# Float32r warm-up products, and a list scheduler's prices set to measured ones, in a one-core decoder layer

## The chip, the cores and the metric

The kernel runs on one core of a Trainium2 chip. The metric is the device time of one execution in microseconds (us), lower is better; a comparison goes by the median of several executions. TensorE (PE) multiplies matrices into PSUM, VectorE (DVE), ScalarE (ACT) and GpSimd (POOL) do elementwise work, and SyncE (SP) issues most of the DMA transfers.

## The reference

One decoder layer over 256 positions of width 1024, all in float32: four groups of attention heads in parallel, cross attention into 256 memory tokens, a squared-ReLU MLP, and a last norm.

```python
def hybrid_mixer(h, w_in, g_group, sinks, w_out, rel_table):
    proj = (h @ w_in).astype(jnp.float32)
    ...
    ya = dilated_attention(heads(aq), heads(ak), heads(av), rel_table)
    yb = stick_breaking_attention(heads(bq), heads(bk), heads(bv))
    yc = sliding_window_sink_attention(heads(cq), heads(ck), heads(cv), sinks, rel_table)
    yd = moba_attention(heads(dq), heads(dk), heads(dv), rel_table)
    groups = []
    for y in (ya, yb, yc, yd):
        y = y.transpose(0, 2, 1, 3).reshape(B, S, -1)
        groups.append(y * lax.rsqrt(jnp.mean(y * y, axis=-1, keepdims=True) + NORM_EPS))
    y = jnp.concatenate(groups, axis=-1) * g_group.astype(jnp.float32)
    return y.astype(h.dtype) @ w_out

def reference(x, mem, rel_table, g_mix, w_in, g_group, sinks, w_out, g_cross, g_mem,
              w_xq, w_xkv, w_xo, g_mlp, w_up, w_down, g_final):
    for l in range(DEPTH):
        x = x + hybrid_mixer(rmsnorm(x, g_mix[l]), w_in[l], g_group[l], sinks[l], w_out[l], rel_table)
        x = x + memory_cross_attention(rmsnorm(x, g_cross[l]), rmsnorm(mem, g_mem[l]),
                                       w_xq[l], w_xkv[l], w_xo[l])
        x = x + squared_relu_mlp(rmsnorm(x, g_mlp[l]), w_up[l], w_down[l])
    return rmsnorm(x, g_final)
```

## The kernel before

All weights stream from HBM once, in units of 256 columns or rows, each in two transfers of 512 KB into one of four `raw` tiles (line 299, issued by SyncE). ScalarE copies a raw tile to float32r (`hi`, line 313), VectorE subtracts that from the raw one (`lo`, line 314), and each product is made of three float32r products, hi·hi, hi·lo and lo·hi (`mm3`, lines 420 to 422). The raw tile is free again when both have read it, and only then can SyncE load the next weight into it.

The order of work on every engine comes from a planner written in Python (`Plan`). Each call of `pe`, `act`, `dve`, `pool` or `dma` adds an operation with an engine, a price in us, what it reads and what it writes. `arrange` simulates the engines: in each step it looks for each engine at the operations whose inputs are there, takes those that could start within a small slack of the earliest, and among them the one of highest rank. The rank is the length of the chain that hangs on it (level plus boost), or a fixed number. The result is one static order for each engine. `FIRST` holds the plan time at which each engine can begin. Two tags, `raw` and `w`, are handed out strictly in the order in which their tiles were made (`FIFO`). At run time each engine works through its own order and waits by semaphores, so a price that is wrong moves the order, and not the work.

At the start, x arrives in two halves of 128 rows (`load_x`). TensorE transposes each half (line 403), VectorE multiplies by the gain (line 413), and ScalarE and VectorE split the result (lines 396, 397). Until x is there, TensorE runs `WARM` products on a zeroed tile (`warm_up`, line 365), whose rank is -1, so that they only fill holes; nothing reads them. They are there for TensorE's clock. The norm's factor is made in parallel: a sum of squares on ScalarE (line 388), a small operation on VectorE (line 382), and a power of -0.5 on GpSimd (line 383, in `rstd_of`). For the two halves of x the factors are spread over all partitions by two transposes (line 455), and ScalarE makes `rk` and `rq` of them (lines 458, 459), with which q and k of every head group are scaled (line 506).

The first head group's values go by line 491, one product at a time, so that each half of x and each half of the weight can be used as it comes. Its q and k (units aq, ak) and all other projections go by `proj_T` and `proj`. The next head group's q (unit bq) follows. Scores are line 633 for the first 128 queries and lines 600 and 601 for the others, the probabilities are transposed by line 535 and multiplied with the values by line 553. GpSimd writes the biases' strip to DRAM (line 469) and reads it back skewed (`toeplitz`, line 713). From about 160 us on the MLP runs alone.

Of the kernel before, what the change touches and what calls it, by code (L numbers as in the profile page):

```python
# [11 lines left out]
F32 = mybir.dt.float32  # L12
F32R = mybir.dt.float32r
# [14 lines left out]
MLP_RANK = 20.0  # L28
LEAD = 0.6
NPRE = 1  # L30
WARM = 30
FRONT = 20.0
EARLY = 1.0
NUDGE = 0.5
# [51 lines left out]
class Plan:  # L86
# [3 lines left out]
    CROSS = 0.2  # L90
    FIFO = ("raw", "w")
    DMA = 0.95
    FIRST = {"DMA": 1.7, "PE": 1.1, "ACT": 0.6, "DVE": 0.6, "POOL": 0.6}
    REFILL = 1.1
    SLACK = {"DVE": 0.3, "ACT": 0.4, "PE": 0.15}
    IDLE = 50.0
# [118 lines left out]
def trunk(ctx: ExitStack, tc: tile.TileContext, a: dict, out: bass.AP):  # L215
# [124 lines left out]
    load("av", 0)  # L340
    load_x(1)
    load("av", 1)
    ident, mhalf, warm = buf("ident", [P, P]), buf("mhalf", [P, 1]), buf("warm", [P, 512], BF16)
    pool(0.5, lambda: make_identity(nc, ident.t), [], [ident])
    pool(0.05, lambda: nc.gpsimd.memset(mhalf.t, -0.5), [], [mhalf])
    dve(512, lambda: nc.vector.memset(warm.t, 0.0), [], [warm])
    onehot, rel, smask = buf("q", [32, STRIP], F32, 2), buf("rel", [32, NROW]), buf("k", [NROW, STRIP], F32, 2)
    sink, nsink = buf("sink", [P, 4]), buf("nsink", [P, 4])
    pool(0.05, lambda: nc.gpsimd.memset(rel.t, 0.0), [], [rel])
# [10 lines left out]
    def warm_up(n):  # L360

        wps = acct()
        plan.fixed = -1.0
        for _ in range(n):
            pe(0.11, lambda: nc.tensor.matmul(wps[:, 0:P], warm[:, 0:P], warm[:, 0:P], start=True, stop=True), [warm], [wps])
        plan.fixed = None

    warm_up(WARM)
# [8 lines left out]
    gains_T(0)  # L377


    def rstd_of(ssq, n):  # L380
        v, r = buf("var", [P, 1], F32, 4), buf("rstd", [P, 1], F32, 16)
        dve(1, lambda: nc.vector.tensor_scalar(v.t, ssq.t, 1.0 / n, EPS, op0=ALU.mult, op1=ALU.add), [ssq], [v])  # L382
        pool(0.5, lambda: nc.gpsimd.tensor_tensor(r.t, v.t, mhalf.t, op=ALU.pow), [v, mhalf], [r])  # L383
        return r

    def rstd_row(src, view, n):
        sq, ssq = buf("sq", [P, D], BF16, 1), buf("ssq", [P, 1], F32, 4)
        act(n, lambda: nc.scalar.activation(sq[:, 0:n], view(), AF.Square, accum_out=ssq.t), [src], [sq, ssq], 1)
        return rstd_of(ssq, n)

    def pair(tag, n, bufs):
        return tuple(buf(tag + x, [P, n, S], F32R, bufs) for x in ("hi", "lo"))
# [36 lines left out]
    def proj_T(dst, view, u, i, hT):  # L429

        for k in range(KB):
            w, j = wt(u, k)
            pe(0.327, lambda w=w, j=j, k=k: mm3(view(), both(w, ALL, j, tsl(i)), both(hT, ALL, k, ALL), k == 0, k == KB - 1),
               [*w] + [(z, (t, k // 4)) for z in hT for t in range(2)], [dst])

    def proj(dst, view, u, hT, t):

        for k in range(KB):
            w, j = wt(u, k)
            pe(0.327, lambda w=w, j=j, k=k: mm3(view(), both(hT, ALL, k, tsl(t)), both(w, ALL, j), k == 0, k == KB - 1),  # L440
               [*w] + [(z, (t, k // 4)) for z in hT], [dst])


# [1 line left out]
    r1 = []  # L445
    for t in range(2):
        gained_T(xt[t], 0, h1, t)
        r1.append(rstd_row(xt[t], lambda t=t: xt[t].t, D))

    rq, rk = buf("rq", [P, S]), buf("rk", [P, S])  # L450
    pr = pst()
# [20 lines left out]
    def project(gi):  # L472
        n = "abcd"[gi]
        q, k = buf("q", [P, 2, S], F32, 2), buf("k", [P, 2, S], F32, 2)
        names = (n + "q", n + "k" if gi != 2 else "ckv")
        v = buf("v4", [P, 2, 4, E + 1], F32, 2) if gi != 2 else buf("v2", [P, 2, 2, E + 1])
        pool(0.1, lambda: nc.gpsimd.memset(v[:, :, :, E:E + 1], 1.0), [], [(v, 0), (v, 1)])

        def values():
            if gi:  # L480
                load(n + "v")
            for t in range(2):
                pv = acct()
                if gi:
                    proj(pv, lambda pv=pv: pv[:, 0:256], n + "v", h1, t)
                else:
                    for half in range(2):
                        for p in ((0, 0), (1, 0), (0, 1)):
                            for kk in range(4 * half, 4 * half + 4):
                                w, j = wt("av", kk)  # L490
                                pe(0.109, lambda p=p, kk=kk, w=w, j=j, t=t, pv=pv: nc.tensor.matmul(
                                    pv[:, 0:256], h1[p[0]][:, kk, tsl(t)], w[p[1]][:, j], start=kk == 0 and p == (0, 0),
                                    stop=kk == KB - 1 and p == (0, 1)), [w[p[1]], (h1[p[0]], (t, half))], [pv])
                act(256, lambda t=t, pv=pv: nc.scalar.activation(
                    v[:, t, :, 0:E], pv[:, 0:256].rearrange("p (h e) -> p h e", h=4), AF.Copy, scale=r1[t].t),
                    [pv, r1[t]], [(v, t)], 1)

        if gi == 0:
            values()
        for u, z, r in zip(names, (q, k), (rq, rk)):  # L500
            if u != "aq":
                load(u)
            acc = acct()
            for i in range(2):
                proj_T(acc, lambda acc=acc, i=i: acc[:, i * S:(i + 1) * S], u, i, h1)
            dve(512, lambda z=z, r=r, acc=acc: nc.vector.tensor_tensor(
                z.t, acc.t.rearrange("p (i t) -> p i t", i=2), r[:, None, :].to_broadcast([P, 2, S]), op=ALU.mult),
                [acc, r], [z])
        if gi == 2:
            pt = pst()  # L510
            transpose(pt, k, lambda: k[:, 1, :], 2, [k])
            for t in range(2):
                act(128, lambda t=t: nc.scalar.activation(
                    v[:, t, :, 0:E], pt[:, tsl(t)].rearrange("p (g e) -> p g e", g=2), AF.Copy), [pt], [(v, t)])
        elif gi:
            values()
        return q, k, v
# [25 lines left out]
    def weigh(pT, v, kv, vkeys):  # L543

        py = pst()

        def view():
            return py[:, 0:4 * (E + 1)].rearrange("p (h e) -> p h e", h=4)

        for h in range(4):  # L550
            def go(h=h):
                for j, (z, i) in enumerate(pT[h]):
                    nc.tensor.matmul(view()[:, h, :], z[:, i, :], v[:, j, kv(h), :], start=j == 0, stop=j == len(pT[h]) - 1)  # L553
            pe(0.205 * len(pT[h]), go, [z for z, _ in pT[h]] + vkeys, [py])
        return py, view

    def divided(py, view, extra=None):
# [51 lines left out]
    def attend(gi, t, q, k, v, yT):  # L609
# [7 lines left out]
        if t:  # L617
            ks, qs = stack_k(k, lambda: k.t, 1 if gi == 2 else 2), stack_q(q, lambda: q[:, :, tsl(1)])
            for half in range(2):
                def go(half=half):  # L620
                    for h in range(4):
                        qi, ki, hf = place(h)
                        if hf == half:
                            stacked(zv(half, qi), qs, 2 * qi + half, ks, 2 * ki + half)
                pe(0.436, go, [*qs, ks], [pz[half]])
        else:
            def go():
                for i in range(2):
# [70 lines left out]
    def rows_mm(acc, hl, u, t, c0, c1, first, last):  # L699

        for j in range(2):
            w, k = wt(u, j)
            pe(0.65 * (c1 - c0) / 512, lambda w=w, k=k, j=j: mm3(
                acc[:, 0:c1 - c0], both(hl, ALL, j, tsl(t)), both(w, ALL, k, slice(c0, c1)), first and j == 0, last and j == 1),
               [*w] + [(z, t) for z in hl], [acc])

# [63 lines left out]
    for t in range(2):  # L770
# [15 lines left out]
        for half in range(2):  # L786
            def go(half=half, pzs=pzs, qs=qs):
                for g in range(2):
                    stacked(pzs[half][:, g * S:(g + 1) * S], qs, 2 * g + half, kx, 2 * g + half)
            pe(0.436, go, [*qs, kx], [pzs[half]])  # L790
        for half, pz in enumerate(pzs):
            dve(512, lambda half=half, pz=pz, nm=nm: nc.vector.tensor_reduce(
                nm[:, half::2], pz.t.rearrange("p (g s) -> p g s", g=2), axis=mybir.AxisListType.X, op=ALU.min),
# [136 lines left out]
```

## Time and profile before

| | us |
|---|---|
| median of 3 runs | 351.68 |
| lowest, highest | 351.62, 352.77 |
| the profiled execution | 352.86 |
| its span, first to last instruction | 350.9 |

The profiled execution is one of its own, 1.2 us above the median; 1.96 us of it lie around the span. PE is busy for 339.3 us, the loads of its stationary operand (PEld) for 313.8 us, DVE for 230.2 us, ACT for 193.8 us and POOL for 25.8 us. A row of the timeline gives the start in us, the duration in us of all instructions that were merged into it, the engine, line, operation, output and inputs, and the count; brackets behind it hold the idle time of the engine just before, and what ended it. Matmuls overlap in the array, so the time from one to the next is the duration of a row less the length of one, divided by the count less one.

### The profile page before, as it was taken

Reading aid. Unit: us, or ns where it says so; the run is one execution under the profiler, and the core shown is the slowest. Engines: PE = TensorE matmul, PEld = TensorE weight load, DVE = VectorE, ACT = ScalarE, POOL = GpSimd, SP = SyncE. Lnnn points to the kernel's source line nnn. Section 1 sums busy time; section 2 is a strip of 40 time slices with the busy share of each in tenths; the row PEclk is TensorE's granted clock in tenths of the full one; section 3 lists DMA queues with packets and bytes.
Section 4 is the critical chain, followed back from the end, with each engine's and each line's share of the span. In section 5 each row is a group of like instructions: output and inputs, shape, how many; then the busy total and the mean of one; then the engine's idle time right before and its main releaser. Section 6 shows DMA issues by size and latency. Waiting matters only on the chain.

```text
span 350.9 us, 6140 instructions
## 1 busy us (share of the span) xinstructions
PE 339.3 (97%) x2442; PEld 313.8 (89%) x2442; DVE 230.2 (66%) x370; ACT 193.8 (55%) x313; POOL 25.8 (7%) x46
## 2 busy tenths in 40 slices
PE   7898999999999999999999999999999999999992
PEld 6798999999898889988999999999999999999982
DVE  3855879589996699788764645555464644555254
ACT  6576857378893467866644443535344443535132
POOL 6440000000201005000100000000000000000000
PEclk9999999999999999999999999999999999999998
DMA  8998574730156435832647554655647555562003
GB/s 269 335 333 248 163 217 143 241 121 0 63 177 183 122 119 180 269 122 91 223 140 238 179 183 145 216 191 181 196 157 235 182 179 155 205 224 78 2 0 120
DMA packets 39900, 59.88 MB, mean 171 GB/s; under 512 B 2006, under 2 KB 33040, under 8 KB 39872
## 3 DMA queue, kind: packets, MB, share of 16 engines
q1 hardware_dynamic: 39216, 57.69, 51.3%
q0 software_dynamic: 640, 1.80, 1.6%
q8 instruction: 19, 0.31, 0.4%
q14 instruction: 9, 0.07, 0.1%
q10 hardware_dynamic: 16, 0.00, 0.0%
HBM read 58.42 MB, written 1.07 MB: 170 GB/s over the span
## 4 chain that ended last, share of the span: by engine, by line
PE 79%; DVE 6%; DMA 6%; ACT 4%; issue 2%; SPq 0%; POOLq 0%; POOL 0%; DVEq 0%; ACTq 0%
PE acc L420 13%; PE acc L421 13%; PE acc L422 13%; PE ps L421 11%; PE ps L422 11%; PE ps L420 11%; DMA raw<-in_w_in_dram 4%; PE ps L553 3%; PE ps L403 3%; DMA x<-in_x_dram 2%; DVE w L314 2%; ACT ks L581 1%; PE ps L535 1%; ACT w L673 1%; ACT qs L593 1%
## 5 line engine op out<-in xcount | busy, mean ns | idle before, releaser
L314 DVE TENSOR_TENSOR w<-raw,w 128x1024 fp32r<-128x1024 f32 x100 | 120.5, 1222 | 85.0 <-ACT w L313 81.6
L313 ACT ACTIVATE w<-raw 128x1024 fp32r<-128x1024 f32 x100 | 103.5, 1057 | 94.2 <-PE ps L421 43.1
L421 PE MATMUL ps<-hTlo,w 128*128 128x256 f32 x256 | 72.0, 281 | 0.0
L420 PE MATMUL ps<-hThi,w 128*128 128x256 f32 x256 | 71.9, 281 | 0.0
L422 PE MATMUL ps<-hThi,w 128*128 128x256 f32 x256 | 71.9, 281 | 0.0
L420 PE MATMUL acc<-w,yThi 128*128 128x512 f32 (+1 forms) x168 | 64.1, 381 | 0.0
L422 PE MATMUL acc<-w,yTlo 128*128 128x512 f32 (+1 forms) x168 | 62.7, 373 | 0.0
L421 PE MATMUL acc<-w,yThi 128*128 128x512 f32 (+1 forms) x168 | 62.6, 373 | 0.0
L420 PEld LDWEIGHTS ps<-hThi,w 128*128 128x128 f32 x256 | 48.2, 188 | 0.1
L422 PEld LDWEIGHTS ps<-hThi,w 128*128 128x128 f32 x256 | 48.3, 189 | 0.0
L421 PEld LDWEIGHTS ps<-hTlo,w 128*128 128x128 f32 x256 | 48.1, 188 | 0.1
L422 PEld LDWEIGHTS acc<-w,yTlo 128*128 128x128 f32 x168 | 31.5, 188 | 6.2
L422 PE MATMUL acc<-hThi,w 128*128 128x256 f32 x128 | 36.0, 281 | 1.0 <-DVE w L314 1.0
L420 PE MATMUL acc<-hThi,w 128*128 128x256 f32 x128 | 36.6, 286 | 0.0
L421 PEld LDWEIGHTS acc<-w,yThi 128*128 128x128 f32 x168 | 31.6, 188 | 5.4
L420 PEld LDWEIGHTS acc<-w,yThi 128*128 128x128 f32 x168 | 31.6, 188 | 5.3
L421 PE MATMUL acc<-hTlo,w 128*128 128x256 f32 x128 | 36.1, 282 | 0.0
L422 PEld LDWEIGHTS acc<-hThi,w 128*128 128x128 f32 x128 | 24.2, 189 | 1.4 <-DVE w L314 1.4
L383 POOL TENSOR_TENSOR rstd<-var,mhalf 128x1 f32<-128x1 f32 x16 | 14.9, 932 | 143.2 <-DVE var L382 99.2
L420 PEld LDWEIGHTS acc<-hThi,w 128*128 128x128 f32 x128 | 24.1, 188 | 0.4
L421 PEld LDWEIGHTS acc<-hTlo,w 128*128 128x128 f32 x128 | 24.1, 188 | 0.0
L834 ACT ACTIVATE q<-ps 128x512 f32<-128x512 f32 x15 | 9.0, 600 | 11.8 <-PE ps L422 11.8
(152 smaller groups left out, 519.0 us busy)
## 6 DMA issues: line engine op xcount, KB each, us to landing
raw<-in_w_up_dram SPq DMA_DIRECT2D x32, 512.0 KB, 3.9
raw<-in_w_down_dram SPq DMA_DIRECT2D x32, 512.0 KB, 3.9
raw<-in_w_in_dram SPq DMA_DIRECT2D x22, 512.0 KB, 5.0
raw<-in_w_out_dram SPq DMA_DIRECT2D x8, 512.0 KB, 3.4
raw<-in_w_xkv_dram SPq DMA_DIRECT2D x4, 512.0 KB, 3.6
w<-dstrip POOLq DMA_DIRECT2D x3, 512.0 KB, 9.2
x<-in_x_dram SPq DMA_DIRECT2D x2, 512.0 KB, 5.9
tmp<-in_mem_dram SPq DMA_DIRECT2D x2, 512.0 KB, 5.5
```

The costliest lines, as they stand in the source:

```text
L313: act(1024, lambda raw=raw, hi=hi: nc.scalar.activation(hi.t, raw.t, AF.Copy), [raw], [hi])
L314: dve(1024, lambda raw=raw, hi=hi, lo=lo: nc.vector.tensor_sub(lo.t, raw.t, hi.t.bitcast(F32)), [raw, hi], [lo])
L383: pool(0.5, lambda: nc.gpsimd.tensor_tensor(r.t, v.t, mhalf.t, op=ALU.pow), [v, mhalf], [r])
L403: nc.tensor.transpose(dst[:, tsl(k)], view()[:, tsl(k)], ident.t)
L420: nc.tensor.matmul(dst, lh, rh, start=start, stop=False)
L421: nc.tensor.matmul(dst, lh, rl, start=False, stop=False)
L422: nc.tensor.matmul(dst, ll, rh, start=False, stop=stop)
L535: nc.tensor.transpose(pt[:, tsl(i)], w[:, h, tsl(j)], ident.t)
L553: nc.tensor.matmul(view()[:, h, :], z[:, i, :], v[:, j, kv(h), :], start=j == 0, stop=j == len(pT[h]) - 1)
L581: act(n * S, lambda own=own, at=at: nc.scalar.activation(ks[own, at, :], view()[own, 0:n, :], AF.Copy), [k], [(ks, half)])
L593: act(256, lambda r=r, own=own, at=at: nc.scalar.activation(qs[r, at, :], view()[own], AF.Copy), [q], [(qs, half)])
L834: act(512, lambda: nc.scalar.activation(r.t, pu.t.rearrange("p (i t) -> p i t", i=2), AF.Relu), [pu], [r])
```

## The change

The warm-up products are of float32r, 128 columns, and there are 15 of them, not 30. The tile that they read is 128 x 128 of float32r and not 128 x 512 of bf16, and its memset is priced accordingly. In the planner's table, a warm-up product is priced at 0.213 for 0.11; three products of 256 columns at 0.355 for 0.327, of 512 columns at 0.70 for 0.65; a single one at 0.1185 for 0.109; scores at 0.48 for 0.436; a product with the values at 0.224 for 0.205. The first transfer can begin at 2.0 for 1.7. The power on GpSimd is priced at 1.0 for 0.5, and for the two halves of x at 1.5 and 3.0. The last norm's power (line 889) stays at 0.5. The prices of ScalarE and VectorE stay.

```diff
-WARM = 30
+WARM = 15
...
-    FIRST = {"DMA": 1.7, "PE": 1.1, "ACT": 0.6, "DVE": 0.6, "POOL": 0.6}
+    FIRST = {"DMA": 2.0, "PE": 1.1, "ACT": 0.6, "DVE": 0.6, "POOL": 0.6}
...
-    ident, mhalf, warm = buf("ident", [P, P]), buf("mhalf", [P, 1]), buf("warm", [P, 512], BF16)
+    ident, mhalf, warm = buf("ident", [P, P]), buf("mhalf", [P, 1]), buf("warm", [P, P], F32R)
...
-    dve(512, lambda: nc.vector.memset(warm.t, 0.0), [], [warm])
+    dve(128, lambda: nc.vector.memset(warm.t.bitcast(F32), 0.0), [], [warm])
...
-            pe(0.11, lambda: nc.tensor.matmul(wps[:, 0:P], warm[:, 0:P], warm[:, 0:P], start=True, stop=True), [warm], [wps])
+            pe(0.213, lambda: nc.tensor.matmul(wps[:, 0:P], warm.t, warm.t, start=True, stop=True), [warm], [wps])
...
-    def rstd_of(ssq, n):
+    def rstd_of(ssq, n, cost=1.0):
...
-        pool(0.5, lambda: nc.gpsimd.tensor_tensor(r.t, v.t, mhalf.t, op=ALU.pow), [v, mhalf], [r])
+        pool(cost, lambda: nc.gpsimd.tensor_tensor(r.t, v.t, mhalf.t, op=ALU.pow), [v, mhalf], [r])
...
-            pe(0.327, lambda w=w, j=j, k=k: mm3(view(), both(w, ALL, j, tsl(i)), both(hT, ALL, k, ALL), k == 0, k == KB - 1),
+            pe(0.355, lambda w=w, j=j, k=k: mm3(view(), both(w, ALL, j, tsl(i)), both(hT, ALL, k, ALL), k == 0, k == KB - 1),
...
-        r1.append(rstd_row(xt[t], lambda t=t: xt[t].t, D))
+        r1.append(rstd_row(xt[t], lambda t=t: xt[t].t, D, 1.5 * t + 1.5))
...
-                                pe(0.109, lambda p=p, kk=kk, w=w, j=j, t=t, pv=pv: nc.tensor.matmul(
+                                pe(0.1185, lambda p=p, kk=kk, w=w, j=j, t=t, pv=pv: nc.tensor.matmul(
...
-            pe(0.205 * len(pT[h]), go, [z for z, _ in pT[h]] + vkeys, [py])
+            pe(0.224 * len(pT[h]), go, [z for z, _ in pT[h]] + vkeys, [py])
...
-                pe(0.436, go, [*qs, ks], [pz[half]])
+                pe(0.48, go, [*qs, ks], [pz[half]])
...
-            pe(0.65 * (c1 - c0) / 512, lambda w=w, k=k, j=j: mm3(
+            pe(0.70 * (c1 - c0) / 512, lambda w=w, k=k, j=j: mm3(
```

The same two new prices stand in `proj` (0.355) and in the scores of the cross attention (0.48).

## Rows read from the trace of the kernel before

**Rows 1.** Busy time by stage; the first row names the columns.
```profile
core 0: us, PE busy (x) PEld busy (x) DVE busy (x) ACT busy (x) POOL busy (x), PEclk, DMA share, GB/s
0.00:29.00 29.00, 26.03 (x195) 24.11 (x196) 16.29 (x27) 17.82 (x28) 13.32 (x27) 1.00 0.96 315
35.00:160.00 125.00, 123.81 (x937) 114.91 (x936) 104.51 (x208) 85.50 (x167) 9.88 (x13) 1.00 0.50 153
160.00:338.00 178.00, 178.00 (x1238) 164.93 (x1237) 97.02 (x106) 82.32 (x101) 1.42 (x4) 1.00 0.51 165
```

**Rows 2.** Timeline of TensorE, start to 11 us.
```profile
1.18 2.74 PE L365 MATMUL acc<-warm 128*128 128x128 bf16 x24 [1.18 <-DVE warm L346]
4.39 1.09 PE L403 MATMUL ps<-ident,x 128*128 128x128 f32 x4 [0.47 <-DMA x<-in_x_dram]
...
6.52 0.85 PE L365 MATMUL acc<-warm 128*128 128x128 bf16 x6
7.63 1.97 PE L403 MATMUL ps<-ident,x 128*128 128x128 f32 x8 [0.26 <-DMA x<-in_x_dram]
9.25 1.07 PE L491 MATMUL acc<-w,hThi 128*128 128x256 f32 x4
10.25 0.81 PE L467 MATMUL ps<-q,rel 32*13 32x384 f32 x2
```

**Rows 3.** Lengths of single products in ns (min/median/max; mean), and later transposes.
```profile
L403 PE MATMUL ps<-ident,x x48: 270/273/477, 4.4 to 164.4; 128*128 128x128 f32 x48
...
L467 PE MATMUL ps<-q,rel 32*13 32x384 f32 x2 | 0.8, 485 | 0.0
...
114.68 1.03 PE L403 MATMUL ps<-ident,tmp 128*128 128x128 f32 x8
```

**Rows 4.** Where TensorE waits in the front, by the timeline.
```profile
17.15 0.32 PE L455 MATMUL ps<-ident,rstd 128*128 128x128 f32 x1 [1.06 <-POOL rstd L383]
...
29.96 0.38 PE L422 MATMUL acc<-hThi,w 128*128 128x256 f32 x1 [0.47 <-DVE w L314]
...
33.02 0.39 PE L422 MATMUL acc<-hThi,w 128*128 128x256 f32 x1 [0.54 <-DVE w L314]
```

**Rows 5.** Timeline of GpSimd, its first two powers.
```profile
7.67 1.41 POOL L383 TENSOR_TENSOR rstd<-var,mhalf 128x1 f32<-128x1 f32 x1 [2.22 <-DVE var L382]
...
14.06 3.04 POOL L383 TENSOR_TENSOR rstd<-var,mhalf 128x1 f32<-128x1 f32 x1
```

**Rows 6.** Timeline of ScalarE, 27 us to 36 us.
```profile
27.59 1.06 ACT L313 ACTIVATE w<-raw 128x1024 fp32r<-128x1024 f32 x1 [1.48 <-DMA raw<-in_w_in_dram]
30.64 1.06 ACT L313 ACTIVATE w<-raw 128x1024 fp32r<-128x1024 f32 x1 [2.00 <-DMA raw<-in_w_in_dram]
...
34.23 1.26 ACT L673 ACTIVATE w<-w,nm 128x128 f32<-128x128 f32 x4
```

**Rows 7.** The chain that ended last, from 16 us: start us, us, what.
```profile
16.68 13.88 DMA raw<-in_w_in_dram
```

**Rows 8.** Timeline of VectorE, start to 30 us.
```profile
0.85 0.27 DVE L346 MEMSET warm<- 128x256 uint32 x1 [0.85 <-PEq L918]
5.92 1.53 DVE L413 TENSOR_TENSOR tmp<-ps,gT 128x512 f32<-128x512 f32 x2 [4.80 <-ACT gT L375]
...
7.43 1.22 DVE L314 TENSOR_TENSOR w<-raw,w 128x1024 fp32r<-128x1024 f32 x1
...
13.18 3.47 DVE L314 TENSOR_TENSOR w<-raw,w 128x1024 fp32r<-128x1024 f32 x3
...
29.82 0.69 DVE L506 TENSOR_TENSOR k<-acc,rk 128x512 f32<-128x512 f32 x1
```

**Rows 9.** Timeline of TensorE: products of 256 columns, and the first scores.
```profile
17.68 0.28 PE L420 MATMUL acc<-hThi,w 128*128 128x256 f32 x1
...
18.03 0.28 PE L420 MATMUL acc<-hThi,w 128*128 128x256 f32 x1
...
30.98 0.72 PE L633 MATMUL ps<-k,q 64*128 64x128 f32 x8
```

More of the change, by code (lines that the diff above doesn't have):

```diff
@@ L377, in trunk, with rstd_row @@
     gains_T(0)
-    def rstd_of(ssq, n):
+    def rstd_of(ssq, n, cost=1.0):
         v, r = buf("var", [P, 1], F32, 4), buf("rstd", [P, 1], F32, 16)
         dve(1, lambda: nc.vector.tensor_scalar(v.t, ssq.t, 1.0 / n, EPS, op0=ALU.mult, op1=ALU.add), [ssq], [v])
-        pool(0.5, lambda: nc.gpsimd.tensor_tensor(r.t, v.t, mhalf.t, op=ALU.pow), [v, mhalf], [r])
+        pool(cost, lambda: nc.gpsimd.tensor_tensor(r.t, v.t, mhalf.t, op=ALU.pow), [v, mhalf], [r])
         return r
-    def rstd_row(src, view, n):
+    def rstd_row(src, view, n, cost=1.0):
         sq, ssq = buf("sq", [P, D], BF16, 1), buf("ssq", [P, 1], F32, 4)
         act(n, lambda: nc.scalar.activation(sq[:, 0:n], view(), AF.Square, accum_out=ssq.t), [src], [sq, ssq], 1)
-        return rstd_of(ssq, n)
+        return rstd_of(ssq, n, cost)
     def pair(tag, n, bufs):
@@ L439, in proj @@
             w, j = wt(u, k)
-            pe(0.327, lambda w=w, j=j, k=k: mm3(view(), both(hT, ALL, k, tsl(t)), both(w, ALL, j), k == 0, k == KB - 1),
+            pe(0.355, lambda w=w, j=j, k=k: mm3(view(), both(hT, ALL, k, tsl(t)), both(w, ALL, j), k == 0, k == KB - 1),
                [*w] + [(z, (t, k // 4)) for z in hT], [dst])
@@ L789, in go @@
                     stacked(pzs[half][:, g * S:(g + 1) * S], qs, 2 * g + half, kx, 2 * g + half)
-            pe(0.436, go, [*qs, kx], [pzs[half]])
+            pe(0.48, go, [*qs, kx], [pzs[half]])
         for half, pz in enumerate(pzs):
```

## The prediction

> **What bounds the kernel now.** I read the table of stages first [rows 1]: from 160 us to 338 us TensorE is busy without a gap, and from 35 us to 160 us it lacks 1.2 us. Busy time is modelled, but no order of work can gain much there. What is left lies in the first 35 us, in the gaps of the attention stages, and in the last 13 us, which hold the output's scaling and store and are not touched.
>
> In the front, three things are to be seen. First, TensorE runs at half pace until about 10 us, though the granted clock of that stretch is given as 1.00 [rows 1]. Four transposes of x take 1.09 us there [rows 2]; eight take 1.03 us at 114.7 us. [...] Second, TensorE stands still for 1.1 us before line 455, waiting for the rstd of the second half of x from GpSimd [rows 4, 5]. Third, it waits at 29.96 us and 33.02 us for a split weight tile, 0.5 us each [rows 4], which comes late because ScalarE had to wait for the transfer (1.48 us and 2.00 us) [rows 6]. The chain of waits says the same: one transfer from 16.68 us to its landing 13.88 us later [rows 7]. It is slow because the DMA engines are full, with a share of 0.96 over the first 29 us [rows 1].
>
> **The change, part by part. Warm-up.** Thirty bf16 products go, fifteen of float32r come. The old ones: 24 in 2.74 us, 0.11 us each [rows 2]. No row shows a float32r product of 128 columns. The low end is the bf16 one, 0.11 us. The high end is that it costs as a plain f32 product: line 467 makes one of 384 columns in two instructions of 0.485 us, both in 0.81 us, so 0.325 us apart and 0.65 us a product, just after the pace had doubled [rows 2, 3]; a third of it is 0.22 us, at half pace 0.43 us. The value I take is 0.213 us: four f32 transposes, of the same shape and word, go at that pace in the same stretch. Fifteen are then 3.2 us. The memset before them writes 128 words a row, not 256 (0.27 us now [rows 8]), so they start about 0.1 us sooner, at 1.1 us, and end at 4.3 us. x lands at about that time (its transposes start at 4.39 us) [rows 2]. So the fifteen fit into the hole, and the path gets 0. At 0.11 us they leave a hole of 1.6 us, also 0. At 0.43 us they last until 7.5 us, and that is a rival below.
>
> The six products at 6.52 us have no successor, since all fifteen are used up. TensorE is idle there until the second half of x lands at 7.6 us [rows 2]: 0 on the path.
>
> **Clock.** In the kernel before, the pace doubled between 9.3 and 10.3 us, with the first real products of line 491: four of 256 columns in 1.07 us, over 0.2 us each [rows 2], and later such a product takes 0.118 us [rows 9]. With denser warm-up it may come sooner: then the eight transposes at 7.63 us take 1.03 us and not 1.97 us [rows 2, 3], 0.9 us less. It may come later: each product of line 491 costs 0.1 us more while it lasts. I take 0; the ends are -0.9 us and +2.8 us (28 products), both ahead of holes of 1.3 us and 1.5 us that swallow most of it.
> [...]
>
> **Prices of GpSimd.** The planner took 0.5 us for a pow. The rows say 1.41 us and 3.04 us for the two halves of x [rows 5]. Both lie under VectorE's line 314: three of them from 13.18 us to 16.65 us, and the pow, issued at 14.06 us, ends at 17.10 us, 0.45 us behind them; the first one ends 0.43 us behind the line 314 that runs to 8.65 us [rows 5, 8]. So the new 1.5 and 3.0 are mostly the neighbour's length, and hold as long as VectorE's order there stays.
>
> With 3.0 the planner knows that line 455 can't run at 16 us. Its TensorE list has the rest of line 491 and 48 products of aq to put ahead (the first is issued at 17.68 us [rows 9]), so the stall goes: 1.06 us idle [rows 4] and the restart of the pipe, 0.27 us [rows 3], 1.3 us. The waits behind it, rk and rq on ScalarE, are not needed until aq is done, 48 x 0.118 = 5.7 us on.
>
> **What is late next.** After aq and ak (96 products at 0.118 us [rows 9], 11.3 us) TensorE needs bq, whose halves reach ScalarE at 27.59 us and 30.64 us [rows 6]. No byte of that is cheaper now, and the DMA engines are full. The 1.3 us therefore go into a longer wait for bq, but for what else can run in it: the scores of line 633 (eight instructions in 0.72 us, now at 30.98 us [rows 9]; 0.6 us of it on TensorE's path). Their k was copied behind line 314 of bq, at 29.82 us [rows 8]; with ak done 1.3 us earlier it is copied ahead of it. The rest of that head group needs ScalarE, which sits in order behind bq's second half until 31.7 us [rows 6]. So I count -0.6 us, with ends 0 and -1.3 us.
>
> **Prices of TensorE.** Three products of 256 columns cost 0.35 us (17.68 us to 18.03 us) [rows 9], and the table now says 0.355 for 0.327; so the filler that the planner puts ahead of a dependent product is true to length, 8% shorter in count. ScalarE and VectorE stay cheap: four of line 673 take 1.26 us, 0.31 us each [rows 6], where the table has 0.24; a line 314 in a run of three takes 1.16 us [rows 8] for 1.14. For the two attention stages, 35 us to 160 us, the table of stages leaves 1.2 us of TensorE idle [rows 1]. A truer TensorE can remove some, a shorter cover can add some: I take 0, with ends -1.2 us and +3 us (the working is with the rival). The rest (later pows at 1.0, DMA first at 2.0 for 1.7) moves plan times by a few tenths; the first x does land as the 2.0 has it: 2.0 + 1.46 + 0.95 = 4.4 us beside 4.39 us [rows 2].
>
> **Sum.** The profiled execution has a span of 350.9 us in 352.86 us; the median is 351.68 us. 350.9 - 0.6 = 350.3 us of span, 352.3 us for such an execution, and 351.1 us at the median.
>
> **Rivals.** (a) *The front moves as a whole.* If the new order also frees the raw tiles sooner, or puts bq's transfer ahead of those of mem or bias, the 1.3 us stay, the two holes of 0.5 us and their restarts (0.27 us of pipe each, so 1.5 us) [rows 3, 4] shrink, and half of the 1.2 us in attention goes: -1.3 - 1.0 - 0.6 = -2.9 us, 348.8 us. For it: the table now carries the length of the stall at line 455. Against it: the full DMA engines.
> (b) *Shorter cover.* From the scores at 30.98 us to the end of the four exponentials at 35.5 us [rows 6, 9] a head group's chain through VectorE and ScalarE takes 4.5 us; with the transposes, values and norm behind it I estimate 9 us. Its filler loses 8%, 0.7 us. Eight such chains of the four groups and two of the cross attention stand between 31 us and 160 us. Where the cover just suffices now, each pays 0.7 us; with half of them, +3.5 us, less 0.6: 354.6 us. It decides from the point at which a dependent product is issued before its operand is there; the waits of lines 553 and 535 tell. For it: the unequal table above. Against it: 1.2 us idle in 125 us now [rows 1], so there is room.
> (c) *Slow warm-up.* At 0.43 us, x's transposes start 3.1 us late, VectorE's first work moves from 5.92 us [rows 8] with them, and VectorE's line of work ends at 16.65 us; the raw tiles come free later, and bq lands up to 3 us later: 354 us.
> (d) *Nothing gained.* The order keeps line 455 ahead, or the clock rises later, and its 2.8 us are taken out of the 1.3 us at line 455 and the 1.5 us at bq: 351.7 us. [...]
>
> **How the numbers follow.** The forecast 0.30, and (d), which the measurement can't tell from it, 0.16, together 0.46; its own range is 349.9 to 352.8 us. (a) 0.28, (b) 0.18, (c) 0.08. A measurement of this kernel tells about 0.5%, 1.8 us, from no change. Faster by more comes from (a), slower from (b) and (c): 0.28, 0.46, 0.26. The range takes in (a) and most of (b): 348.4 to 354.6 us.
>
> **What would show it.** Right: fifteen products at 0.21 us ending near 4.3 us; no wait at line 455; bq's ScalarE splits still near 27.6 us and 30.6 us; TensorE after 160 us as dense as now. Wrong: warm products at 0.11 or 0.43 us; bq's splits over 1 us away; waits of lines 553 and 535 that add up to more than 2 us; the pace still half at 11 us.

## The result

The changed kernel takes 355.86 us (median of four, 354.56 to 357.23) beside 352.17 us for the kernel before (four, 351.62 to 352.77): 1.0105 times as long, with an interval of 1.0061 to 1.0149. A second measurement of it, with an execution's trace of its own, gave 1.0086 (1.0062 to 1.0111); that is the run after_pair below. The prediction was 351.1 us, faster by a little. It is slower by 1%, and no rival in the list has the mechanism.

The profiled execution took 354.56 us, the shortest of its four, with a span of 352.2 us. Busy time by stage, with the columns of [rows 1]:

```profile
0.00:29.00 29.00, 26.29 (x164) 24.05 (x165) 16.55 (x27) 18.73 (x29) 13.33 (x27) 1.00 0.95 309
35.00:160.00 125.00, 122.76 (x935) 114.40 (x934) 102.22 (x204) 84.36 (x167) 10.66 (x13) 1.00 0.46 147
160.00:338.00 178.00, 178.00 (x1240) 164.96 (x1240) 97.91 (x108) 82.34 (x102) 2.17 (x4) 1.00 0.52 166
```

Behind 160 us nothing has changed. From 35 us to 160 us TensorE lacks 2.24 us, where it lacked 1.19 us. TensorE's timeline of the front, which answers to [rows 2, 4, 9]:

```profile
1.04 3.46 PE L365 MATMUL acc<-warm 128*128 128x128 f32 x15 [1.04 <-DVE warm L346]
4.30 1.07 PE L403 MATMUL ps<-ident,x 128*128 128x128 f32 x4
...
8.29 1.97 PE L403 MATMUL ps<-ident,x 128*128 128x128 f32 x8 [1.67 <-DMA x<-in_x_dram]
...
15.36 1.05 PE L491 MATMUL acc<-w,hThi 128*128 128x256 f32 x4
...
17.14 1.07 PE L491 MATMUL acc<-w,hThi 128*128 128x256 f32 x8
...
24.48 0.38 PE L455 MATMUL ps<-ident,rstd 128*128 128x128 f32 x2
...
31.75 0.71 PE L633 MATMUL ps<-k,q 64*128 64x128 f32 x8
```

The warm-up is as forecast: (3.46 - 0.48) / 14 = 0.213 us a product (0.48 us: the longest of the transposes of that shape, [rows 3]). It is over when x is there: the transposes behind it start at 4.30 us without a wait. Line 455 comes behind aq at 24.5 us, and its wait is gone. The pace doubles late: products of line 491 are (1.05 - 0.41) / 3 = 0.213 us apart at 15.4 us and (1.07 - 0.28) / 7 = 0.113 us at 17.1 us (0.41 and 0.28 us: the lengths of one at either pace in this trace). The trace's record of the granted clock begins at 16.41 us, with 1.00; in the kernel before it begins at 10.04 us, with 1.00 too. "Full" below is a granted clock of 1.00 in this record. The scores of line 633 start 0.77 us later than in [rows 9].

GpSimd's two powers, as in [rows 5]:

```profile
7.57 1.41 POOL L383 TENSOR_TENSOR rstd<-var,mhalf 128x1 f32<-128x1 f32 x1 [2.12 <-DVE var L382]
...
14.72 3.04 POOL L383 TENSOR_TENSOR rstd<-var,mhalf 128x1 f32<-128x1 f32 x1
```

VectorE around the copy of k, as in [rows 8]:

```profile
26.20 1.22 DVE L314 TENSOR_TENSOR w<-raw,w 128x1024 fp32r<-128x1024 f32 x1
...
29.55 1.22 DVE L314 TENSOR_TENSOR w<-raw,w 128x1024 fp32r<-128x1024 f32 x1
30.91 0.69 DVE L506 TENSOR_TENSOR k<-acc,rk 128x512 f32<-128x512 f32 x1
```

and ScalarE, as in [rows 6]:

```profile
21.48 2.95 ACT L313 ACTIVATE w<-raw 128x1024 fp32r<-128x1024 f32 x3
...
28.11 1.07 ACT L313 ACTIVATE w<-raw 128x1024 fp32r<-128x1024 f32 x1
30.98 1.06 ACT L313 ACTIVATE w<-raw 128x1024 fp32r<-128x1024 f32 x1 [1.80 <-DMA raw<-in_w_in_dram]
...
32.31 1.27 ACT L581 ACTIVATE ks<-k 64x512 fp32r<-64x512 f32 x2
...
34.57 1.27 ACT L673 ACTIVATE w<-w,nm 128x128 f32<-128x128 f32 x4
```

Here the new order shows. Three more rows of the kernel before go with [rows 6, 8], one of VectorE and two of ScalarE:

```profile
28.68 1.23 DVE L314 TENSOR_TENSOR w<-raw,w 128x1024 fp32r<-128x1024 f32 x1 [2.24 <-ACT w L313]
```

```profile
20.30 2.00 ACT L313 ACTIVATE w<-raw 128x1024 fp32r<-128x1024 f32 x2
...
31.97 1.27 ACT L581 ACTIVATE ks<-k 64x512 fp32r<-64x512 f32 x2
```

The rows don't name the unit of a weight; it follows from the order in which the tiles are loaded. By that count the kernel before splits two tiles (ak) in the row at 20.30 us, bq's halves at 27.59 us and 30.64 us, then rounds k (line 581), which makes of k the operand of the later scores. The exponentials of the first scores (line 673) stand behind it in ScalarE's order. The changed one splits three (ak and bq's first half) from 21.48 us, bq's second half at 28.11 us, then *bk's* first half at 30.98 us, for which it waits 1.80 us, and only then rounds k. VectorE likewise: k is copied behind the subtraction of bq's *second* half (29.55 us), in the kernel before behind that of the first (28.68 us). The new plan has both engines do one weight tile more ahead of k of head group a.

The planner's own times say why. They belong to no profile:

```
plan, us                           before          after
VectorE, copy of k                 25.37           26.65
VectorE, bq's second half          25.97           25.47
ScalarE, rounding of k             26.17           27.45
ScalarE, split of bk's first half  27.16           25.75
```

With the new prices, mostly those of TensorE, ak ends 1.28 us later in the plan, and k with it. Bq's second half and bk's first half land only 0.3 us later, so that VectorE and ScalarE now find them ready while k isn't. These were near ties, two operations of one engine that could start at almost the same plan time, and they turn over. On the chip the weights come much later than planned: bq's second half is split at 28.11 us and not 24.29 us, bk's first half at 30.98 us and not 25.75 us.

### The profile page after: what moved, and what is told of

Same layout as the page of the kernel before. It is cut to its first block, busy times and chain, and to the rows that moved or that the text cites. A ratio compares the mean times of both kernels' runs of the same rounds, so it can differ in the third digit from the quotient of the medians.

```text
span 352.2 us, 6125 instructions
## 1 busy us (share of the span) xinstructions
PE 340.7 (97%) x2427; PEld 315.4 (90%) x2427; DVE 229.7 (65%) x369; ACT 193.4 (55%) x314; POOL 27.4 (8%) x46
## 3 DMA queue, kind: packets, MB, share of 16 engines
HBM read 58.42 MB, written 1.07 MB: 169 GB/s over the span
## 4 chain that ended last, share of the span: by engine, by line
PE 81%; ACT 7%; DVE 5%; DMA 4%; issue 2%; SPq 0%; POOLq 0%; POOL 0%; ACTq 0%; DVEq 0%
PE acc L420 13%; PE acc L422 13%; PE acc L421 13%; PE ps L422 11%; PE ps L420 11%; PE ps L421 11%; PE ps L553 3%; PE ps L403 3%; PE acc L491 2%; DMA raw<-in_w_in_dram 2%; DMA x<-in_x_dram 2%; ACT w L313 1%; DVE w L314 1%; PE ps L535 1%; ACT w L673 1%
## 5 line engine op out<-in xcount | busy, mean ns | idle before, releaser
L383 POOL TENSOR_TENSOR rstd<-var,mhalf 128x1 f32<-128x1 f32 x16 | 16.4, 1027 | 140.7 <-DVE var L382 130.9
```

What stands on the lines that cost most here:

```text
L383: pool(cost, lambda: nc.gpsimd.tensor_tensor(r.t, v.t, mhalf.t, op=ALU.pow), [v, mhalf], [r])
```

## The experiments

All kernels compute everything, and the warm-up products are read by nothing. Ratios are to executions of the kernel before on the same chip at the same time, with a 95% interval. Each run has one trace, of one execution, and times read from it hold for that execution.

**before_warm15: the warm-up alone.** The order of the kernel before; the first fifteen warm-up products are of float32r, the others left out.

```diff
...
-        for _ in range(n):
-            pe(0.11, lambda: nc.tensor.matmul(wps[:, 0:P], warm[:, 0:P], warm[:, 0:P], start=True, stop=True), [warm], [wps])
+        for i in range(n):
+            pe(0.11, (lambda: nc.tensor.matmul(wps[:, 0:P], warm.t, warm.t, start=True, stop=True)) if i < 15 else None, [warm], [wps])
```

> The kernel before with all its prices and its order; of its thirty warm-up products the first fifteen are float32r in the first hole, and none stand in the second. Theory C: full pace at about 16 us and a time of 354 to 356 us. Theory O: the pace may come late, the time stays within 1 us of the kernel before, about 352 us.

352.68 us, 1.0011 (0.9989 to 1.0033). Full pace comes at 15.15 us, 5 us later than in the trace of before, and costs nothing that can be measured.

**before_no_six: the later six products alone.** The kernel before with `if i < 24 else None` in the same place.

> The kernel before with its 24 bf16 warm-up products in the first hole and without the six in the second. Theory C in the form that the six are what counts: full pace at about 16 us, 354 to 356 us. Theory C in the form that the type counts (float32r less than bf16): full pace near 10 us and about 352 us. Theory O: about 352 us whatever the pace does.

352.70 us, 1.0007 (0.9983 to 1.0030). The clock was full from 4.30 us to 7.71 us and again from 11.13 us. The loss of the six costs nothing that can be measured either.

**prices_only: the new prices with the old warm-up.**

```diff
...
-            pe(0.213, lambda: nc.tensor.matmul(wps[:, 0:P], warm.t, warm.t, start=True, stop=True), [warm], [wps])
+            pe(0.11, lambda: nc.tensor.matmul(wps[:, 0:P], warm[:, 0:P], warm[:, 0:P], start=True, stop=True), [warm], [wps])
```

> The new prices (products, powers, first transfer) with the old warm-up: thirty bf16 products priced at 0.11, the old memset. Theory C: the pace comes near 10 us if some products still fall into the hole before the second half of x, and the time is 351 to 353 us. Theory O: 355 to 356 us.

355.40 us, 1.0089 (1.0061 to 1.0116): the loss comes with the prices, and so with the order that they make. In its trace the clock was full early, from 5.27 us, and TensorE begins aq at 14.83 us, in the changed kernel's trace at 19.18 us. TensorE's timeline:

```profile
27.18 0.28 PE L422 MATMUL acc<-hThi,w 128*128 128x256 f32 x1
32.06 0.78 PE L633 MATMUL ps<-k,q 64*128 64x128 f32 x8 [4.60 <-DVE k L506]
...
33.15 0.41 PE L421 MATMUL acc<-hTlo,w 128*128 128x256 f32 x1
...
36.09 0.28 PE L420 MATMUL acc<-hThi,w 128*128 128x256 f32 x1
```

Its chain of waits (start, us, what), which names each link:

```profile
15.94 13.13 DMA raw<-in_w_in_dram
29.09 1.06 ACT w L313
30.18 0.35 DVE w L314
...
31.32 0.69 DVE k L506
32.06 0.78 PE ps L633 x8
```

A transfer of 13.1 us, the split, the subtraction, the copy of k, the scores. K itself could have been copied some 4 us sooner, since TensorE's last product ahead of the wait is the one at 27.18 us. And the busy time (as in rows 1) shows the granted clock around the wait of 4.6 us, the figure before the DMA share:

```profile
29.00:31.00 2.00, 0.00 (x0) 0.00 (x0) 0.82 (x1) 1.49 (x2) 0.00 (x0) 1.00 0.98 312
31.00:33.00 2.00, 0.94 (x9) 0.75 (x10) 2.00 (x3) 1.92 (x4) 0.00 (x0) 0.90 0.36 99
33.00:35.00 2.00, 2.00 (x10) 2.00 (x11) 1.91 (x11) 1.98 (x5) 0.00 (x0) 0.50 0.81 265
35.00:38.00 3.00, 3.00 (x24) 3.00 (x23) 2.21 (x5) 2.13 (x4) 0.00 (x0) 0.83 0.49 157
```

It falls from 1.00 to 0.50 at 32.58 us, 0.5 us behind the wait, and is back at 35.99 us; at 0.50 a product takes 0.41 us and not 0.28 us, and the next one starts 0.21 us after it and not 0.12 us.

**fill8: the changed kernel with eight more warm-up products** in the hole ahead of the second half of x.

```diff
...
-            transpose(pt, x, lambda n=n: x[:, nsl(n)], 4, [(x, n)])
+            transpose(pt, x, lambda n=n: x[:, nsl(n)], 4, [(x, n)], 8 * (x is xt[0] and g == 0 and n == 1))
```

> The changed kernel in its own order, with eight more float32r warm-up products behind the first half of x's transposes, in the hole of 1.7 us before the second half lands (8 x 0.213 = 1.7 us). Theory C (the clock): the full pace comes near 10 us as before, not at 16.4 us, and the time falls by 2 to 4 us to about 352.5 us. Theory O (the new order costs): full pace may come earlier, the time stays at 355 to 356 us.

356.07 us, 1.0104 (1.0071 to 1.0137). In its trace the clock was full from 10.69 us, and no time is won. TensorE comes to the scores early, and waits as in prices_only; the granted clock is 0.50 from 31.17 us, within the wait, to 37.99 us:

```profile
33.24 1.23 PE L636 MATMUL ps<-k,q 64*128 64x128 f32 x8 [4.08 <-DVE k L509]
```

In this trace, then, what the earlier clock gains is waited away.

**p_pe: the prices of TensorE alone.** The kernel before with 0.355, 0.1185, 0.224, 0.48 and 0.70.

> The kernel before with the new prices of TensorE's products alone. In its order the copies of q and of k both stand behind the subtraction of bq's second half. Theory K: a wait of 4 us or more for them and 354.5 to 357 us. Rival R: the price of the powers is what matters, 352 us.

356.32 us, 1.0117 (1.0094 to 1.0141). By itself this part costs as much as the whole change. VectorE has both q and k of head group a behind the subtraction, which waits 2.85 us for the split:

```profile
31.20 1.23 DVE L314 TENSOR_TENSOR w<-raw,w 128x1024 fp32r<-128x1024 f32 x1 [2.85 <-ACT w L313]
32.35 0.68 DVE L506 TENSOR_TENSOR q<-acc,rq 128x512 f32<-128x512 f32 x1
32.95 0.68 DVE L506 TENSOR_TENSOR k<-acc,rk 128x512 f32<-128x512 f32 x1
```

The scores start at 33.68 us, 2.7 us later than in [rows 9], and TensorE then waits 1.07 us for the exponentials of the same chain. The wait of 4 us or more that I expected isn't there. Between 35 us and 160 us it is busy for 121.50 us, 2.3 us less than in [rows 1]; 1.1 us of that lie ahead of 60 us.

**p_rstd: the prices of the powers alone.** The kernel before with 1.0, 1.5 and 3.0.

> The kernel before with the new prices of GpSimd's powers alone (1.0; 1.5 and 3.0 for x). In its order the copy of k stands behind the subtraction of bq's second half too. Theory K: a wait of some 3 us at line 633 and 354 to 356 us. Rival R: it only takes the stall at line 455 out, 351 us.

353.74 us, 1.0056 (1.0031 to 1.0080). This is just below the 354 us that I expected, and the wait of 3 us at line 633 isn't there. The wait at line 455 goes, and other waits take its place, for weights:

```profile
23.87 0.38 PE L420 MATMUL acc<-hThi,w 128*128 128x256 f32 x1 [0.98 <-ACT w L313]
25.13 0.39 PE L422 MATMUL acc<-hThi,w 128*128 128x256 f32 x1 [0.76 <-DVE w L314]
```

**fix_after and fix_prices: one edge added to the plan.** The planner is told that the subtraction of bq's second half reads head group a's k, so k's copy must come first. The chip needs no such wait; it only moves the order.

```diff
...
-                dve(1024, lambda raw=raw, hi=hi, lo=lo: nc.vector.tensor_sub(lo.t, raw.t, hi.t.bitcast(F32)), [raw, hi], [lo])
+                dve(1024, lambda raw=raw, hi=hi, lo=lo: nc.vector.tensor_sub(lo.t, raw.t, hi.t.bitcast(F32)),
+                    [raw, hi] + (hold if (u, part) == ("bq", 1) else []), [lo])
```

> The changed kernel with one edit: in the planner, VectorE's subtraction of the second half of bq is said to read the first head group's k, so it is ordered behind the copy of k and not ahead of it; the rest of the order stays. Theory K (the copy of k waits behind that subtraction, which waits for its transfer; TensorE stands at the scores of line 633 and the clock falls): no wait over 1 us at line 633, no stretch at half pace after 17 us, and 352 to 353.5 us. Rival R (the cost lies in the rest of the new order, from 75 us on): 355 us or more.

> The same edit on the new prices with the old bf16 warm-up. Theory K: the wait of 4.6 us at line 633 and the half pace behind it go, and the time falls from 355.4 us to 351.5 to 353 us. Rival R: 355 us.

353.28 us, 1.0023 (1.0004 to 1.0042), for the changed kernel with this edge; 352.62 us, 1.0014 (0.9992 to 1.0037), for prices_only with it. Most of the loss is gone, with every new price in place. The edge moves more than it names: in the new plan ScalarE rounds k ahead of the split of bk's first half, and TensorE works off bq's second half ahead of bk's first. No run separates these moves. VectorE in the trace of fix_after, whose lines stand one lower there:

```profile
30.80 0.69 DVE L507 TENSOR_TENSOR k<-acc,rk 128x512 f32<-128x512 f32 x1 [1.26 <-PE acc L423]
31.41 1.22 DVE L314 TENSOR_TENSOR w<-raw,w 128x1024 fp32r<-128x1024 f32 x1
```

and ScalarE:

```profile
29.95 1.07 ACT L313 ACTIVATE w<-raw 128x1024 fp32r<-128x1024 f32 x1 [2.02 <-DMA raw<-in_w_in_dram]
...
31.52 1.28 ACT L582 ACTIVATE ks<-k 64x512 fp32r<-64x512 f32 x2
32.83 1.06 ACT L313 ACTIVATE w<-raw 128x1024 fp32r<-128x1024 f32 x1
33.80 1.26 ACT L674 ACTIVATE w<-w,nm 128x128 f32<-128x128 f32 x4
```

VectorE now waits for ak itself, not for a weight. k is rounded at 31.52 us, not 32.31 us, and the exponentials start at 33.80 us, not 34.57 us.

**fix_fill8: this edge with the eight more products**, so with an early clock (full from 12.08 us).

> The changed kernel with the copy of k forced ahead, and with the eight more warm-up products of fill8 in the hole before x's second half. Theory K: where the full pace comes early (by 11 us), TensorE reaches the scores of line 633 by 29 us and does not stand there for 4 us; no stretch at half pace between 27 us and 40 us; 351 to 353 us against 356.1 us of fill8. Rival (an early clock alone makes a long wait behind aq and ak whatever the order): a wait over 3 us and 355 us.

353.22 us, 1.0017 (1.0002 to 1.0032), where fill8 without the edge had 1.0104. k is copied at 28.99 us, the scores start at 29.83 us without a wait, and the granted clock stays at 1.00 from 20 us to 100 us:

```profile
29.83 0.72 PE L637 MATMUL ps<-k,q 64*128 64x128 f32 x8
```

**after_pair and fix_pair: the changed kernel unaltered, and fix_after, side by side.**

> The changed kernel unaltered, on the same chip as the next run. If the cost is k's copy behind the subtraction of bq's second half, executions in which TensorE reaches full pace early show a wait of over 2 us before the scores of line 633 and a fall of the clock behind it, and the median is 355.5 to 356.5 us; an execution that reaches full pace late (16 us) shows no wait there and is among the fastest. Rival, that the cost lies in the stages behind 35 us alone: no wait at line 633 in any execution, whatever the clock did, and the median still 355 us or more.

> The same kernel with k's copy ordered ahead of that subtraction. If that order is the cost, the median is 2 to 3.2 us below the run beside it, on the same chip, and no execution shows a wait at the scores. Rival: less than 1 us below.

355.41 us, 1.0086 (1.0062 to 1.0111), beside 353.26 us, 1.0029 (1.0012 to 1.0047): the edge is worth 2.15 us. But one half of what I expected fell. This execution of the changed kernel had a late clock (15.68 us) and no wait at the scores, as expected, and yet it took 355.57 us, above the median. So the wait at the scores is not how the changed kernel itself loses in the two executions that have a trace. In this one, ScalarE's timeline shows another way:

```profile
31.80 1.06 ACT L313 ACTIVATE w<-raw 128x1024 fp32r<-128x1024 f32 x1 [2.58 <-DMA raw<-in_w_in_dram]
...
33.12 1.27 ACT L581 ACTIVATE ks<-k 64x512 fp32r<-64x512 f32 x2
...
35.39 1.27 ACT L673 ACTIVATE w<-w,nm 128x128 f32<-128x128 f32 x4
```

and TensorE waits for the same tile, bk's first half:

```profile
32.91 0.39 PE L420 MATMUL acc<-hThi,w 128*128 128x256 f32 x1 [0.21 <-ACT w L313]
...
34.17 0.39 PE L422 MATMUL acc<-hThi,w 128*128 128x256 f32 x1 [0.76 <-DVE w L314]
```

In these traces a tile ahead of k holds it up: with an early clock on VectorE, where TensorE then waits 4 us and more for the scores, with a late one on ScalarE. In after_pair TensorE lacks 0.97 us between 29 us and 35 us, in the first trace of the changed kernel only 0.11 us. Both ways show in the start of the first four exponentials (line 673 in the kernel before), here for one execution of each kernel:

| kernel | clock full from, us | k rounded, us | exponentials, us | ratio |
|---|---|---|---|---|
| before | 10.04 | 31.97 | 34.23 | 1 |
| before_warm15 | 15.15 | 30.84 | 33.11 | 1.0011 |
| p_first | 4.03 to 7.44, 17.68 | 32.48 | 34.76 | 0.9973 |
| p_rstd | 10.44 | 33.91 | 35.20 | 1.0056 |
| after | 16.41 | 32.31 | 34.57 | 1.0105 |
| after_pair | 15.68 | 33.12 | 35.39 | 1.0086 |
| fill8 | 10.69 | 33.22 | 35.49, at half clock | 1.0104 |
| prices_only | 5.27 | 32.04 | 34.31, at half clock | 1.0089 |
| fix_after | 16.38 | 31.52 | 33.80 | 1.0023 |
| fix_pair | 17.04 | 31.84 | 34.11 | 1.0029 |
| fix_fill8 | 12.08 | 31.30 | 33.56 | 1.0017 |

The column doesn't rank the kernels: p_first, the fastest by its median, starts the exponentials later in its trace than the changed kernel does. A trace shows where k stands in the order; what that costs is told by the medians. In the pair 0.5 us of the 2.15 us lie outside the span, and the rest ahead of 35 us, as far as busy time tells: between 35 us and 160 us TensorE lacks 2.24 us in after_pair and in fix_pair alike, and from there to 338 us nothing in either.

**fix_front: the rest.** fix_after with the old prices of TensorE for the output projection, the cross attention and the MLP.

> The changed kernel with the copy of k forced ahead, and with the old prices for the products of the output projection, the cross attention and the MLP. If what is left of the cost (0.2%) sits in the waits at 143 us and 152 us, they go, and the time is 351.5 to 352.7 us, at or below the kernel before. If it sits at 94 us to 96 us or in the front: 353 to 354 us as fix_after.

352.66 us, 1.0012 (0.9994 to 1.0030). Busy time from 35 us to 160 us, first of fix_after, then of fix_front:

```profile
35.00:160.00 125.00, 122.77 (x934) 114.59 (x934) 102.85 (x206) 85.05 (x167) 10.66 (x13) 1.00 0.48 151
```

```profile
35.00:160.00 125.00, 123.41 (x940) 115.01 (x939) 103.38 (x207) 85.12 (x167) 10.05 (x13) 1.00 0.48 152
```

The old prices give TensorE 0.64 us of busy time back, of the 1.04 us that fix_after lacks beside [rows 1]. The edge left those waits alone (of after, by TensorE's waits: line, for whom, us):

```profile
PE ps L420 <- DVE ks L582: 0.8, 1, 0.8
PE ps L600 <- ACT pT L243: 0.5, 1, 0.5
PE ps L601 <- DVE ql L594: 0.4, 1, 0.4
```

So this is the likely seat of the remaining 0.2%; the times don't separate it (fix_fill8, measured beside it, has 1.0017).

**Truer prices elsewhere, two misses.** dma_true is the changed kernel with the transfer of bq's second half priced four times as long (`2048 if (u, part) == ("bq", 1) else 512`); fix_act is fix_after with ScalarE at 0.17 us and 0.78 ns an element, for 0.02 us and 0.93 ns, and without the 0.1 us that some operations had on top.

> The changed kernel with one more price: the transfer of bq's second half costs four times as much in the planner, so that it lands there at 28.7 us, near the 27.6 to 31.9 us that ScalarE's split of it waited for in the traces, and not at 24.3 us. The planner then puts the copy of k ahead of that split by itself. Theory K, with the price of the transfer as the root: no wait over 1 us at line 633, 352 to 353.5 us, as with the order forced. Rival: the planner finds another bad order, 354 us or more.

> The changed kernel with the copy of k forced ahead, and ScalarE priced by the traces as well (0.17 us + 0.78 ns an element). If the unequal table (TensorE true, ScalarE cheap) is what keeps the forced order from beating the kernel before, 350 to 351.5 us, with smaller waits of lines 420, 535, 600 and 601 after 90 us. If the planner's errors compensate each other, so that each true price alone moves other near ties, 353 us or more.

355.35 us, 1.0071 (1.0044 to 1.0099), and 354.12 us, 1.0044 (1.0023 to 1.0064). With dma_true k does come first, on both engines (rounded at 31.50 us), but bq's second half is now split too late, and TensorE waits 0.7 us for it; between 35 us and 160 us it lacks 2.88 us, and more time lies outside the span (below). So k ahead of the weights is not enough by itself. With fix_act k is copied first, but ScalarE splits bk's first half ahead of k again (rounded at 32.46 us). Its trace has more busy time between 35 us and 160 us (123.58 us) and waits for weights in the front (1.2 us); as it is of the shortest of twelve executions, 352.18 us, it doesn't show where the median loses. Neither bears out the idea that one more price made true puts the order right.

**p_first and first_warm: the small parts.** p_first is the kernel before with the first transfer at 2.0 and nothing else; first_warm has the new warm-up besides.

> The kernel before with the first transfer at 2.0 in place of 1.7 alone. The copy of k stays ahead of the subtraction of bq's second half. Theory K: within 1 us of the kernel before, 351.5 to 353 us. Rival R: this price carries part of the cost, 354 us.

> The change without the new prices of TensorE's products and of GpSimd's powers: the fifteen float32r warm-up products with their price and the first transfer at 2.0 stay. The copy of k stays ahead of the subtraction of bq's second half. Theory K: no wait at line 633 and a time of 351 to 352.5 us, at or below the kernel before. Theory C (the missing six products cost through the clock): 354 us or more.

351.75 us, 0.9973 (0.9955 to 0.9991), and 352.24 us, 0.9988 (0.9971 to 1.0005). These parts do no harm. p_first is the one version below the kernel before, by 0.9 us; with the new warm-up besides this can't be told from no change, so I wouldn't build on it.

## Why the prediction was wrong

**The step that failed is "What is late next".** It says of k that "with ak done 1.3 us earlier it is copied ahead of" line 314 of bq. That takes the order on VectorE as a result of when things are ready on the chip. It is written down beforehand, out of the planner's times, and in these k came later (25.37 to 26.65 us), since TensorE's new prices make ak longer. The -0.6 us counted there became a loss: the edge that undoes the order takes 2.15 us off, side by side, and brings 1.0105 to 1.0023. Nor was the -0.6 us to be had with k in its place: in fix_fill8 the scores start 1.15 us ahead of [rows 9], and the kernel is no faster than before (1.0002 to 1.0032). Between 35 us and 160 us TensorE lacks 2.23 us there too.

**The prices of TensorE** were a term of 0 with an end of +3 us, for shorter cover in the attention stages. Alone they cost 1.17%, some 3.7 us beside 352.58 us (p_pe): past that end. Of the 3.56 us between the spans of the two traces 2.31 us are idle between 35 us and 160 us, 1.08 us of them ahead of 60 us, in the chain behind the late k; the rest, some 1.2 us, lies in the front. The front and this chain the term didn't look at. Rival (b)'s mechanism is there, but small: in the changed kernel 1.05 us more idle in 125 us, of which fix_front gets 0.64 us back, and the waits at lines 535 and 553, by which I meant to tell it, come to 0.6 us. Its 354.6 us lie near the result for another reason.

**The prices of GpSimd** did as forecast at line 455: no wait, powers of 1.41 us and 3.04 us again. What the stall's end was worth was wrong. Alone they make the kernel 0.56% slower (p_rstd); the freed time turned into waits for weights, as the text said, and into more.

**"No byte of that is cheaper now"** was wrong too: bq's halves were split some 4 us (the third tile from 21.48 us) and at 28.11 us, 2.5 us sooner, since the new plan loads bq's first half ahead of the biases. That is rival (a)'s condition. It was met, and the gain didn't come: the next tile in line, bk's first half, took bq's place in front of k.

**Warm-up and clock** were right. A product takes 0.213 us, x's transposes follow at 4.3 us, and before_warm15 puts the ratio at 1.0011 (0.9989 to 1.0033), so rival (c) falls. The clock was later, as rival (d) has it: full from 15.2 to 17.0 us in eight of the nine traces with fifteen float32r products (10.9 us in the ninth), for good from 5.3 to 17.7 us in the seven with bf16, at 10.7 and 12.1 us with the eight more. With one trace of each this is not shown. Nor does a run show what sets the time of the rise. The lack of the six products alone doesn't: before_no_six and the ninth of those traces (fix_act) are without them and were at full pace for good from 11.13 us and 10.87 us, and p_pe, with them, only from 16.80 us. And no kernel here leaves the warm-up out altogether, so what it does for the clock is not shown either. The pace still half at 11 us, which the prediction has among the signs of being wrong, was seen and is not what costs: before_warm15 and first_warm have it, at 1.0011 and 0.9988. "Holes that swallow most of it" held for a late first rise. It isn't shown for a long fall behind an early rise: executions of the kernel before with a mean granted clock of 0.982, as in p_first's trace, took 353.18 us and more, those with 0.990 took 352.28 us and less (last section).

**The case I left out** is a wrong table whose errors cancel. The kernel before prices TensorE 8% too low, and in its plan bq's halves are split at 22.71 us and 23.99 us, where [rows 6] have 27.59 us and 30.64 us: k and the weights are both early, and in the right order to each other. Setting one side right took the balance away.

**What stays open.** A part of the loss lies outside the span. Device time less span is 2.1 to 2.6 us in all executions of after, after_pair, fill8, prices_only and dma_true, and 1.9 to 2.0 us in those of the kernel before and of all other kernels here. That is some 0.5 us of the 2.15 us that the edge takes off; no row shows what it is. dma_true has it with another order, so the place of k doesn't explain it. And that the early clock's wait at the scores happens in the changed kernel itself is argued from fill8 and prices_only; both of its own traces have a late clock. Of its ten executions two have a mean granted clock of 0.987 and 0.988, as fill8's trace has (0.987), and each is the longest of its set (357.23 us, 356.13 us); the others have 0.996 to 0.998. That fits such a wait and a fall of the clock, but where in the execution their clock was low is not on record. And of the gain of the edge ahead of 35 us, the first trace of the changed kernel shows only 0.11 us as a wait between 29 us and 35 us: that the rest lies in the order around k is shown by the edge, not by the rows.

## What to carry to other kernels

When a planner's prices change, print the old and the new order and look first for near ties that turned over, above all where one side waits for a transfer: what has no wait belongs ahead of what has one. A price made true for one engine is no gain while the times of the transfers are still wrong; judge the order, not the table. And a stall that goes is worth only what the next thing in that engine's order can use.

## What the runs showed of the hardware

In both traces with a wait of over 4 us at the scores the granted clock falls from 1.00 to 0.50: behind the wait of 4.60 us, for 3.4 us (prices_only), and within that of 4.08 us, for 6.8 us (fill8). No fall goes with the wait of 1.06 us in [rows 4]: the granted clock is 1.00 from 17 us to 338 us there. As products of 256 columns are 0.21 us apart at 0.50 and 0.12 us at 1.00, I estimate that such a wait costs more than its length: up to nearly half of the stretch at 0.50 goes as well.

When the clock first rises differs by over 11 us between kernels with the same bf16 products in the warm-up: full from 5.27 us in prices_only and from 16.80 us in p_pe. In two kernels it was full at 4.30 us and 4.03 us, fell to 0.50 at 7.71 us and 7.44 us, in a hole of 2.36 us and of 2.65 us, and was full again from 11.13 us (before_no_six) and from 17.68 us (p_first). Executions of one kernel differ too, in the mean granted clock and in time: of 133 executions of the kernel before, the twelve with a mean of 0.982, as in p_first's trace, took 353.18 to 353.54 us, the twelve with 0.990, near before_no_six's 0.989, took 350.83 to 352.28 us. A granted clock of 1.00 ahead of the record's first entry doesn't tell the pace: in the kernel before it is 1.00 over the first 9.2 us, with the entry at 10.04 us, and the eight transposes at 7.63 us are (1.97 - 0.48) / 7 = 0.213 us apart [rows 2, 3], those at 114.68 us (1.03 - 0.27) / 7 = 0.109 us [rows 3].

Ahead of the rise a float32r product of 128 columns took as long as one of 256 columns, in the first trace of the changed kernel: 0.213 us from one to the next for the warm-up (line 365) as for line 491 at 15.4 us.
